# Two transposes inside one pair of products per up stage, and residual additions block by block, in a two-layer encoder

## The chip, the cores and the metric

The kernel runs on one core of one Trainium2 chip. The metric is device time in microseconds, the median of the runs of one kernel. Engines are named as in the profile: PE (TensorE matmul) with PEld (its weight loads), DVE (VectorE), ACT (ScalarE), POOL (GpSimd) and SP (SyncE, which here only issues DMAs).

## The reference, cut to what matters

The program is an encoder trunk of two layers over 256 tokens of width 2048. Each layer is a token mixer and a gated MLP, both added to the residual. The change lies in the MLP alone.

```python
def conv_glu(hn, w_up, conv_w, conv_b, w_down):
    u = hn @ w_up                              # 2048 -> 2 * 5504
    a, v = jnp.split(u, 2, axis=-1)
    ...                                        # width-3 convolution of a along the tokens: c
    return (jax.nn.gelu(c, approximate=False) * v) @ w_down

for layer in range(DEPTH):
    hn = rmsnorm(h, norm_mix_g[layer])
    ...                                        # layer 0: mLSTM mixer, layer 1: HGRN2 mixer
    h = h + mix
    h = h + conv_glu(rmsnorm(h, norm_ffn_g[layer]), ffn_w_up[layer], ffn_conv_w[layer],
                     ffn_conv_b[layer], ffn_w_down[layer])
```

## The kernel before

**Precision.** Every float32 operand is split into a high and a low part (`halves`: L170 on ACT casts the high part `wh`, L171 on DVE subtracts to get the low part `wl`), and a product is a sum of products of parts.

**The MLP in stages.** The 43 blocks of 128 hidden columns are worked in three parts of 16, 16 and 11 blocks (`PARTS`). Part 0, 1 and 2 of a layer each have an *up stage* and then a *down stage*.

**Up stage.** One chunk (kind `fm`) per hidden block, over 16 steps k of the contraction. A step has two blocks of weights, f = 0 (the gate branch) and f = 1 (the value branch), and for each a **pair of products** into one PSUM bank: L441, high weights with 512 moving columns (high and low part of the activations side by side), and L444, low weights with 256 moving columns. A chunk is thus 32 pairs, and an up stage of 16 chunks 512 pairs. PE has nothing else to do in it.

**The `turn` transposes.** At places given by the table `RESETS`, the kernel issues a PE transpose of the identity matrix into a spare bank (`turn`, L428). Nothing reads its result. The table names a chunk of the stage and a step k: chunk 2 and chunk 9 of part 0, chunks 0 and 6 of parts 1 and 2, one transpose each, ahead of a pair.

**Down stage.** Two `Pair` objects, one for each half of the 2048 output columns. A `Pair` multiplies 2x2 blocks by a scheme with seven instead of eight block products (`stream_pair`, products recorded at L309). Its plan is a string such as `PSNSPSNN`: P and S are groups by the scheme, N and H plain products; for S the sums of weights are made on DVE (`T`, L234 to L236), for P they come precomputed from DRAM (`pr`). The products accumulate in two PSUM tiles of two banks, `d0` (its halves are `c12` and `c11`) and `d1` (`c22` and `c21`), and in three banks `m1`, `m6`, `m7`. PSUM holds two such `d` tiles, so the second `Pair` of a stage gets the same two tiles and its first product in `c12` waits until they are read.

**Back into the residual.** After the last scheme group `middle` copies `m1` and `c22` out on ACT (into `s1` and `v5`), forms the remaining sums in a tile `at` on DVE (L1156 to L1158) and adds them to the residual `hx` (L1182, two additions of 1024 columns). `at` is one of the three buffers of the tag `raw`, the same through which the weights arrive from DRAM. At the end of the `Pair`, `done` adds the two `d` tiles to the residual (L1187, two additions of 1024 columns). The last half of the last part uses plain chunks instead of a `Pair`, so there are 11 `Pair`s in all, and the second follows directly on the first in five stages (parts 0, 1, 2 of layer 0; parts 0, 1 of layer 1).

**What sets the order.** The program is built by a tile framework that schedules the instructions of every engine by a simulated timeline and puts in the semaphores. So the order in the source is not the order on an engine, and a change in one place can move instructions in another. Each engine executes its own list in order. SP issues the weight DMAs in order, each when its `raw` buffer is free.

Of the kernel before, what the change touches and what calls it, by code (L numbers as in the profile page):

```python
# [8 lines left out]
F32 = mybir.dt.float32  # L9
# [3 lines left out]
ALU = mybir.AluOpType  # L13
PSUM = bass.MemoryType.PSUM

P = 128
# [2 lines left out]
KT = D // P  # L19
FT = 5504 // P  # L20
PARTS = ((0, 16), (16, 16), (32, 11))
RESETS = (((2, 1), (9, 1)), ((0, 3), (6, 1)), ((0, 3), (6, 1)))
A = "PSNSPSNN"
A2 = "PSNSPSNN"
B = "PSNNNH"
# [24 lines left out]
RAW = 3  # L50
# [15 lines left out]
def trunk_kernel(ctx, tc, xT, x_d, fg_d, pp_d, cst_d, sel_d, w_gate, w_first, w_aq, w_ak, w_av, w_ao, w_aout,  # L66
                 w_bq, w_bv, w_bg, w_bout, w_up, w_down, w_last, out, mscr, sums):
    nc = tc.nc
    act, dve, pool, pe = nc.scalar, nc.vector, nc.gpsimd, nc.tensor

    keep = ctx.enter_context(tc.tile_pool(name="keep", bufs=1))
    wpool = ctx.enter_context(tc.tile_pool(name="wpool", bufs=1))
# [12 lines left out]
    ident = cst[:, C_ID:C_ID + P]  # L85
# [5 lines left out]
    def aux(name):  # L91
        return psa.tile([P, 512], F32, tag="aux", name=name)
# [279 lines left out]
    def stream(chunks):  # L372
        pieces = split_weights(chunks[1:])
        ready = []

        def fetch():
            p = next(pieces, None)
            if p is not None:
                ready.append(p)

        chunks[0].before()
        first_chunk(chunks[0], n0, fetch)
        for ch in chunks[1:]:
            if ch.before:
                ch.before()
            if ch.kind == "pair":
                def take():
                    fetch()
                    return ready.pop(0)
                stream_pair(ch, take)  # L390
                continue
            if ch.apart:
                ps = [aux("mm") for _ in range(2)]
            else:
                d = double("mm")
                ps = [d[:, 0:512], d[:, 512:1024]]
            k = 0
            while k < ch.nk:
                fetch()
                wh, wl, n = ready.pop(0)  # L400
                if ch.last and k + sum(p[2] for p in ready) + n == ch.nk:
                    pieces_, k0 = [(wh, wl, n)] + ready, k
                    for t in range(2):
                        k = k0
                        for wh, wl, n in pieces_:
                            for kk in range(n):
                                x, c = ch.x(k), slice(kk * 512, (kk + 1) * 512)
                                xh, xl = x[:, t * P:(t + 1) * P], x[:, T + t * P:T + (t + 1) * P]
                                pe.matmul(ps[t], xh, wh[:, c], start=False, stop=False)
                                pe.matmul(ps[t], xh, wl[:, c], start=False, stop=False)  # L410
                                pe.matmul(ps[t], xl, wh[:, c], start=False, stop=k == ch.nk - 1)
                                k += 1
                        ch.half(ps[t], t)
                    return
                for kk in range(n):
                    x = ch.x(k)
                    st, sp = k == 0, k == ch.nk - 1
                    if ch.kind != "fm":
                        c = slice(kk * 512, (kk + 1) * 512)
                        for t in range(2):  # L420
                            xh, xl = x[:, t * P:(t + 1) * P], x[:, T + t * P:T + (t + 1) * P]
                            pe.matmul(ps[t], xh, wh[:, c], start=st, stop=False)  # L422
                            pe.matmul(ps[t], xh, wl[:, c], start=False, stop=False)  # L423
                            pe.matmul(ps[t], xl, wh[:, c], start=False, stop=sp)  # L424
                        side.tick(1.3)
                    else:
                        if k == ch.reset:
                            pe.transpose(aux("turn")[:, 0:P], ident, ident)  # L428
                        if k == 1 and ch.turns or side.turned:
                            side.turned = False  # L430
                            cs = [slice(kk * ch.width + f * P, kk * ch.width + (f + 1) * P) for f in range(2)]
                            for f in range(2):
                                pe.matmul(ps[f], wh[:, cs[f]], x, start=st, stop=False)  # L433
                            for f in range(2):
                                pe.matmul(ps[f][:, 0:T], wl[:, cs[f]], x[:, 0:T], start=False, stop=sp)  # L435
                            side.tick(0.65)
                            k += 1
                            continue
                        for f in range(len(ps)):
                            c = kk * ch.width + f * P  # L440
                            pe.matmul(ps[f], wh[:, c:c + P], x, start=st, stop=False)  # L441
                            if f:
                                side.tick(0.325 * len(ps))
                            pe.matmul(ps[f][:, 0:T], wl[:, c:c + P], x[:, 0:T], start=False, stop=sp)  # L444
                    k += 1
            ch.done(ps)
# [643 lines left out]
    def ffn(layer, norm, nxt):  # L1090
# [56 lines left out]
            def form(self, c, kind):  # L1147
                return self.forms[c, kind]

        def combine(acc, at, w):  # L1150
            v5 = ev.tile([P, 512], F32, tag="jk", bufs=1, name="v5")[:, 0:w]
            flat = at.rearrange("p t c -> p (t c)")
            s1, u2, u3 = (flat[:, 512 * i:512 * i + w] for i in range(3))
            act.copy(s1, acc["m1"][:, 0:w])
            act.copy(v5, acc["c22"][:, 0:w])
            dve.tensor_tensor(u2, s1, acc["m6"][:, 0:w], ALU.add)  # L1156
            dve.tensor_tensor(u3, u2, acc["m7"][:, 0:w], ALU.add)
            dve.tensor_tensor(at[:, :, 512:512 + w], flat[:, 512:1536].rearrange("p (a c) -> p a c", a=2)[:, :, 0:w],  # L1158
                              v5.unsqueeze(1).broadcast_to([P, 2, w]), ALU.add)

        for part, (f0, nf) in enumerate(PARTS):
            GT = Gated(nf)
            final = last and part == len(PARTS) - 1
            made = [{} for _ in range(2)]
            ahead = []
            for c in range(1 if final else 2):
                for i, kind in enumerate((DOWN_PLAN, DOWN_PLAN2)[c][nf]):
                    if kind == "P":
                        made[c][i] = numbers.pop()
                        ahead.append((made[c][i], w_down[layer, c][:, (f0 + 2 * i) * 1024:(f0 + 2 * i + 2) * 1024]))  # L1170

            for i in range(nf):
                chunks.append(Chunk("fm", w_up[layer, f0 + i], KT, norm.x, done_up(f0 + i, i, GT, ahead)))
                chunks[-1].reset = dict(RESETS[part]).get(i)
                chunks[-1].apart = bool(part) and i == 0
            for c in (0, 2):
                def middle(acc, c=c):
                    at = wpool.tile([P, 2048], F32, tag="raw", bufs=RAW, name="at").rearrange("p (t c) -> p t c", t=2)
                    combine(acc, at, 512)
                    for t in range(2):  # L1180
                        h = hm[:, t, 512 * c:512 * c + 1024]
                        dve.tensor_tensor(h, h, at[:, t], ALU.add)  # L1182

                def done(acc, c=c, part=part):
                    for t in range(2):
                        h = hm[:, t, 512 * c:512 * c + 1024]
                        dve.tensor_tensor(h, h, acc["rows"][t], ALU.add)  # L1187
                    if part == len(PARTS) - 1:
                        if last or c:
                            end()  # L1190
                        nxt.add(c)
                        nxt.add(c + 1)
                if final and c == 2:
                    continue
                ch = Pair(w_down[layer, c // 2][:, f0 * 1024:(f0 + nf) * 1024], (DOWN_PLAN if c == 0 else DOWN_PLAN2)[nf], GT.get, GT.form, done, middle)
                ch.made, ch.box = made[c // 2], box
                chunks.append(ch)
            if final:
                def done(ps):
                    for t in range(2):  # L1200
                        h = hm[:, t, 1024:1536]
                        dve.tensor_tensor(h, h, ps[t], ALU.add)
                    nxt.add(2)
                for c in (2, 3):
                    chunks.append(Chunk("tm", w_last[c - 2], nf, GT.get, done))
                chunks[-1].last, chunks[-1].half = True, nxt.half
                chunks[-1].apart = chunks[-2].apart = True
# [135 lines left out]
```

## Time and profile before

| | |
|---|---|
| median of 3 runs | 2399.92 us |
| the three runs | 2402.45, 2399.92, 2399.79 us |
| the profiled execution | 2402.44 us, with a span of 2400.4 us from first to last instruction |
| PE busy | 2383.1 us, 99% of the span |
| DVE busy | 1940.4 us, 81% |
| ACT busy | 1338.3 us, 56% |
| mean DMA rate | 226 GB/s over the span |

In the profile a row of the timeline reads: start in us, duration in us, engine, source line, operation, tile written <- tiles read, shape, count; in square brackets the idle time of the engine before it and what ended it. Matmuls are pipelined, so the duration of one is longer than the distance to the next; where rates are meant, the distances between starts are used. A row of the windows view reads: stretch, its length, then per engine the busy time and in brackets the number of instructions, and at the end the granted PE clock, the DMA share and the rate.

### The profile page before, as it was taken

Reading aid. Unit: us, or ns where it says so; the run is one execution under the profiler, and the core shown is the slowest. Engines: PE = TensorE matmul, PEld = TensorE weight load, DVE = VectorE, ACT = ScalarE, POOL = GpSimd, SP = SyncE. Lnnn points to the kernel's source line nnn. Section 1 sums busy time; section 2 is a strip of 40 time slices with the busy share of each in tenths; the row PEclk is TensorE's granted clock in tenths of the full one; section 3 lists DMA queues with packets and bytes.
Section 4 is the critical chain, followed back from the end, with each engine's and each line's share of the span. In section 5 each row is a group of like instructions: output and inputs, shape, how many; then the busy total and the mean of one; then the engine's idle time right before and its main releaser. Section 6 shows DMA issues by size and latency. Waiting matters only on the chain.

```text
span 2400.4 us, 37326 instructions
## 1 busy us (share of the span) xinstructions
PE 2383.1 (99%) x14212; PEld 2037.1 (85%) x14212; DVE 1940.4 (81%) x3197; ACT 1338.3 (56%) x2057; POOL 306.0 (13%) x451
## 2 busy tenths in 40 slices
PE   9999999999999999999999999999999999999998
PEld 7888888888888888888888888888888888887887
DVE  7766655888988888888888888885788888888876
ACT  6655455655556645655555555555565556654554
POOL 0100000111011110101222222220011101110100
PEclk9999999999999999999999999999999999999999
DMA  7655555888778887855455555445698768987854
GB/s 295 203 174 171 191 174 186 272 275 281 268 251 277 287 286 238 292 196 204 172 176 167 168 176 173 165 174 181 223 296 282 262 239 276 293 284 243 260 190 175
DMA packets 106019, 545.84 MB, mean 227 GB/s; under 512 B 10720, under 2 KB 11360, under 8 KB 55280
## 3 DMA queue, kind: packets, MB, share of 16 engines
q1 hardware_dynamic: 66656, 437.34, 53.2%
q0 software_dynamic: 38320, 104.94, 14.5%
q8 instruction: 111, 1.82, 0.3%
q10 hardware_dynamic: 864, 1.19, 0.1%
q14 instruction: 68, 0.56, 0.1%
HBM read 501.41 MB, written 42.01 MB: 226 GB/s over the span
## 4 chain that ended last, share of the span: by engine, by line
PE 96%; DVE 2%; DMA 2%; issue 0%; ACT 0%; SPq 0%; POOLq 0%; POOL 0%; ACTq 0%; DVEq 0%
PE mm L441 36%; PE mm L444 18%; PE c L309 11%; PE mm L422 7%; PE mm L423 7%; PE mm L424 7%; PE m L309 3%; DMA raw<-in_w_down 1%; DVE wl L171 1%; PE mm L433 1%; PE pn L790 1%; PE pd L973 1%; PE py L1022 1%; PE pz L536 0%; PE mm L435 0%
## 5 line engine op out<-in xcount | busy, mean ns | idle before, releaser
L441 PE MATMUL mm<-xt,wh 128*128 128x512 f32 x3690 | 1289.0, 395 | 0.0
L170 ACT CAST wh<-raw 128x1024 fp32r<-128x1024 f32 (+1 forms) x829 | 844.2, 1026 | 794.9 <-PE mm L441 471.7
L171 DVE TENSOR_TENSOR wl<-raw,wh 128x1024 fp32r<-128x1024 f32 (+1 forms) x829 | 989.8, 1199 | 357.8 <-ACT wh L170 351.0
L444 PE MATMUL mm<-xt,wl 128*128 128x256 f32 x3690 | 1027.1, 279 | 0.0
L441 PEld LDWEIGHTS mm<-xt,wh 128*128 128x128 f32 x3690 | 691.8, 188 | 158.4
L444 PEld LDWEIGHTS mm<-xt,wl 128*128 128x128 f32 x3690 | 693.7, 188 | 1.4
L309 PE MATMUL c<-wh,g 128*128 128x512 f32 x666 | 217.5, 390 | 0.0
L422 PE MATMUL mm<-wh,xt 128*128 128x512 f32 x480 | 188.2, 392 | 0.0
L423 PE MATMUL mm<-wl,xt 128*128 128x512 f32 x480 | 187.7, 391 | 0.0
L424 PE MATMUL mm<-wh,xt 128*128 128x512 f32 x480 | 187.3, 390 | 0.0
L309 PEld LDWEIGHTS c<-wh,g 128*128 128x128 f32 x666 | 125.2, 188 | 26.1
L309 PE MATMUL c<-wl,g 128*128 128x512 f32 x333 | 129.9, 390 | 0.0
L424 PEld LDWEIGHTS mm<-wh,xt 128*128 128x128 f32 x480 | 90.2, 188 | 18.5
L422 PEld LDWEIGHTS mm<-wh,xt 128*128 128x128 f32 x480 | 90.1, 188 | 18.5
L423 PEld LDWEIGHTS mm<-wl,xt 128*128 128x128 f32 x480 | 90.2, 188 | 17.4
L476 ACT COPY b<-mm 128x256 f32<-128x256 f32 x236 | 86.4, 366 | 20.5 <-DVE z L477 6.7
L170 ACT CAST wh<-T 128x1024 fp32r<-128x1024 f32 x54 | 55.3, 1050 | 69.7 <-PE c L309 43.3
L262 POOL DMA_DIRECT2D sums<-pr x76 | 53.0, 699 | 293.9 <-ACT pr L259 156.2
L282 POOL DMA_DIRECT2D pr<-sums x76 | 41.3, 551 | 359.5 <-PE c L309 244.5
L171 DVE TENSOR_TENSOR wl<-T,wh 128x1024 fp32r<-128x1024 f32 x54 | 64.8, 1223 | 26.0 <-ACT wh L170 25.7
L249 POOL COPY pr<-a 128x1 f32<-128x1 f32 x38 | 31.1, 819 | 424.2 <-DVE a L482 246.6
L309 PE MATMUL c<-wh,F 128*128 128x512 f32 x178 | 70.2, 394 | 3.8 <-DVE hx L1187 3.8
(274 smaller groups left out, 3022.7 us busy)
## 6 DMA issues: line engine op xcount, KB each, us to landing
raw<-in_w_up SPq DMA_DIRECT2D x172, 1024.0 KB, 5.6
raw<-in_w_down SPq DMA_DIRECT2D x60, 1024.0 KB, 6.1
raw<-in_w_bq SPq DMA_DIRECT2D x48, 1024.0 KB, 4.9
sums<-pr POOLq DMA_DIRECT2D x76, 512.0 KB, 8.1
pr<-sums POOLq DMA_DIRECT2D x76, 512.0 KB, 7.5
pr<-in_w_down POOLq DMA_DIRECT2D x38, 512.0 KB, 6.7
raw<-in_w_ao SPq DMA_DIRECT2D x16, 1024.0 KB, 4.9
raw<-in_w_aout SPq DMA_DIRECT2D x16, 1024.0 KB, 4.8
```

The lines of the kernel that those rows point to most:

```text
L170: act.copy(h, r)
L171: dve.tensor_tensor(l, r, h.bitcast(F32), ALU.subtract)
L249: pool.tensor_copy(b[:, 0, 0:1], after)
L262: pool.dma_start(sums[n, j].rearrange("p (i o b) -> p i o b", i=2, o=2)[:, :, o], v.rearrange("p (i b) -> p i b", i=2))
L282: pool.dma_start(z[j], sums[n, j][:, 1024 * i:1024 * i + 1024])
L309: pe.matmul(o, a, b, start=name not in begun, stop=sp and i == 2)
L422: pe.matmul(ps[t], xh, wh[:, c], start=st, stop=False)
L423: pe.matmul(ps[t], xh, wl[:, c], start=False, stop=False)
L424: pe.matmul(ps[t], xl, wh[:, c], start=False, stop=sp)
L441: pe.matmul(ps[f], wh[:, c:c + P], x, start=st, stop=False)
L444: pe.matmul(ps[f][:, 0:T], wl[:, c:c + P], x[:, 0:T], start=False, stop=sp)
L476: act.copy(b, ps[:, T:2 * T])
```

## The change

In the up stage the table `RESETS` now names one place per part: chunk 2, step 1 in part 0 (as the first entry before), and chunk 0, step 0 in parts 1 and 2. There, two transposes are issued instead of one, after the high product of f = 0 and ahead of its low product, both into one `turn` tile. Two transposes stood in each up stage before (at two places), and two stand there now.

In the down stage, `middle` does without `combine`: the sums are formed and added to the residual in blocks of 512 columns, eight additions of 512 in place of two of 512, one of 2x512 and two of 1024. In `done`, the two halves of `d0` are added each by itself, `c12` first, then `c11`; `d1` is added as a whole as before.

```diff
-RESETS = (((2, 1), (9, 1)), ((0, 3), (6, 1)), ((0, 3), (6, 1)))
+RESETS = ((2, 1), (0, 0), (0, 0))
...
-                        if k == ch.reset:
-                            pe.transpose(aux("turn")[:, 0:P], ident, ident)
...
                             pe.matmul(ps[f], wh[:, c:c + P], x, start=st, stop=False)
                             if f:
                                 side.tick(0.325 * len(ps))
+                            if not f and k == ch.reset:
+                                turn = aux("turn")
+                                for o in (0, P):
+                                    pe.transpose(turn[:, o:o + P], ident, ident)
                             pe.matmul(ps[f][:, 0:T], wl[:, c:c + P], x[:, 0:T], start=False, stop=sp)
...
-        def combine(acc, at, w):
-            v5 = ev.tile([P, 512], F32, tag="jk", bufs=1, name="v5")[:, 0:w]
-            flat = at.rearrange("p t c -> p (t c)")
-            s1, u2, u3 = (flat[:, 512 * i:512 * i + w] for i in range(3))
-            act.copy(s1, acc["m1"][:, 0:w])
-            act.copy(v5, acc["c22"][:, 0:w])
-            dve.tensor_tensor(u2, s1, acc["m6"][:, 0:w], ALU.add)
-            dve.tensor_tensor(u3, u2, acc["m7"][:, 0:w], ALU.add)
-            dve.tensor_tensor(at[:, :, 512:512 + w], flat[:, 512:1536].rearrange("p (a c) -> p a c", a=2)[:, :, 0:w],
-                              v5.unsqueeze(1).broadcast_to([P, 2, w]), ALU.add)
...
                 def middle(acc, c=c):
-                    at = wpool.tile([P, 2048], F32, tag="raw", bufs=RAW, name="at").rearrange("p (t c) -> p t c", t=2)
-                    combine(acc, at, 512)
-                    for t in range(2):
-                        h = hm[:, t, 512 * c:512 * c + 1024]
-                        dve.tensor_tensor(h, h, at[:, t], ALU.add)
+                    at = wpool.tile([P, 2048], F32, tag="raw", bufs=RAW, name="at")
+                    s1, u2, u3 = (at[:, 512 * i:512 * i + 512] for i in range(3))
+                    v5 = ev.tile([P, 512], F32, tag="jk", bufs=1, name="v5")
+                    h11, h12, h21, h22 = (hm[:, t, o:o + 512] for t in range(2) for o in (512 * c, 512 * c + 512))
+                    add = lambda o, a, b: dve.tensor_tensor(o, a, b, ALU.add)
+                    act.copy(s1, acc["m1"])
+                    act.copy(v5, acc["c22"])
+                    add(u2, s1, acc["m6"])
+                    add(h11, h11, s1)
+                    add(u3, u2, acc["m7"])
+                    add(u2, u2, v5)
+                    add(h21, h21, u3)
+                    add(u3, u3, v5)
+                    add(h12, h12, u2)
+                    add(h22, h22, u3)
 
                 def done(acc, c=c, part=part):
-                    for t in range(2):
-                        h = hm[:, t, 512 * c:512 * c + 1024]
-                        dve.tensor_tensor(h, h, acc["rows"][t], ALU.add)
+                    for name, t, o, n in (("c12", 0, 512, 512), ("c11", 0, 0, 512), ("rows", 1, 0, 1024)):
+                        h = hm[:, t, 512 * c + o:512 * c + o + n]
+                        dve.tensor_tensor(h, h, acc["rows"][1] if n == 1024 else acc[name], ALU.add)
```

What the scheduler made of it is seen at three places. The first is PE in part 0 of layer 0, at the end of step 0 and the start of step 1 of chunk 2; `xt_3112` and `xt_3115` are the activations of steps 0 and 1. Before:

```order
L441 MATMUL mm<-xt_3112,wh 128x512
L444 MATMUL mm<-xt_3112,wl 128x256
L428 MATMUL turn<-cst 128x128
L441 MATMUL mm<-xt_3115,wh 128x512
L444 MATMUL mm<-xt_3115,wl 128x256
L441 MATMUL mm<-xt_3115,wh 128x512
```

With the change (L439 and L446 are the two products, L445 the transposes):

```order
L439 MATMUL mm<-xt_3112,wh 128x512
L446 MATMUL mm<-xt_3112,wl 128x256
L439 MATMUL mm<-xt_3115,wh 128x512
L445 MATMUL turn<-cst 128x128 x2
L446 MATMUL mm<-xt_3115,wl 128x256
L439 MATMUL mm<-xt_3115,wh 128x512
```

The transposes moved from between two pairs into a pair, and there are two. The second single transpose of this stage, at chunk 9, is gone. It is the same in layer 1.

The second place is PE at the start of the up stage of part 1 in layer 0, where the last products of the down stage of part 0 (L309) end. Before, the scheduler had drawn both transposes of the stage together and put them behind two high products:

```order
L309 MATMUL c_5788<-wh,g_5459 128x512
L441 MATMUL mm<-xt_3112,wh 128x512 x2
L428 MATMUL turn<-cst 128x128 x2
L444 MATMUL mm<-xt_3112,wl 128x256 x2
L441 MATMUL mm<-xt_3115,wh 128x512
L444 MATMUL mm<-xt_3115,wl 128x256
```

With the change:

```order
L309 MATMUL c_5791<-wh,g_5458 128x512
L439 MATMUL mm<-xt_3112,wh 128x512
L445 MATMUL turn<-cst 128x128 x2
L439 MATMUL mm<-xt_3112,wh 128x512
L446 MATMUL mm<-xt_3112,wl 128x256 x2
L439 MATMUL mm<-xt_3115,wh 128x512
L446 MATMUL mm<-xt_3115,wl 128x256
```

The two transposes now stand one high product earlier, so two low products follow each other without them. Part 2 and layer 1 read the same.

The third place is DVE around the change from the first `Pair` to the second in part 0 of layer 0. `m_...` and `c_...` are the PSUM tiles of the first `Pair`; `wl<-raw` are low parts of weights of both, `T` the sums for the second. Before:

```order
L1158 TENSOR_TENSOR at<-at,v_5711 128x2x512
L171 TENSOR_TENSOR wl<-raw,wh 128x1024
L1182 TENSOR_TENSOR hx<-hx,at 128x1024 x2
L171 TENSOR_TENSOR wl<-raw,wh 128x512
L234 TENSOR_TENSOR T_5801<-raw 128x1024
L1187 TENSOR_TENSOR hx<-hx,c_5462 128x1024
L1187 TENSOR_TENSOR hx<-hx,c_5463 128x1024
L235 TENSOR_TENSOR T_5801<-raw,T_5801 128x512
```

With the change (L1173 are the additions of `middle`, L1188 those of `done`):

```order
L1173 TENSOR_TENSOR hx<-hx,at 128x512 x2
L171 TENSOR_TENSOR wl<-raw,wh 128x1024
L1173 TENSOR_TENSOR at<-at,v_5710 128x512
L171 TENSOR_TENSOR wl<-raw,wh 128x512
L234 TENSOR_TENSOR T_5804<-raw 128x1024
L1173 TENSOR_TENSOR hx<-hx,at 128x512
L1188 TENSOR_TENSOR hx<-hx,c_5461 128x512 x2
L235 TENSOR_TENSOR T_5804<-raw,T_5804 128x512
L1188 TENSOR_TENSOR hx<-hx,c_5462 128x1024
```

Most additions of `middle` moved ahead of the weights that arrive at the change of `Pair`s; one of them stands behind the sum `T`; and the addition of the second `d` tile moved behind the second step of `T`.

More of the change, by code (lines that the diff above doesn't have):

```diff
@@ L1173, in ffn @@
                 chunks.append(Chunk("fm", w_up[layer, f0 + i], KT, norm.x, done_up(f0 + i, i, GT, ahead)))
[L1174 removed]
+                chunks[-1].reset = RESETS[part][1] if i == RESETS[part][0] else None
                 chunks[-1].apart = bool(part) and i == 0
```

## The prediction

> **What bounds the kernel now.** I read first the page, for the busiest engine and for the chain that ended last.
>
> ```profile
> span 2400.4 us, 37326 instructions
> PE 2383.1 (99%) x14212; PEld 2037.1 (85%) x14212; DVE 1940.4 (81%) x3197; ACT 1338.3 (56%) x2057; POOL 306.0 (13%) x451
> PE 96%; DVE 2%; DMA 2%; issue 0%; ACT 0%; SPq 0%; POOLq 0%; POOL 0%; ACTq 0%; DVEq 0%
> ```
>
> PE is busy for 99% of the span. A change that issues the same products can win only by making their distance in time smaller, or by ending one of PE's few waits. So the next view is the windows of the up stages with the high products (L441) alone. One such product starts each pair, so the length of a window over its count is the time of a pair.
>
> ```profile
> 418.20:495.60 77.40, 77.40 (x224) 41.81 (x223) 1.00 0.86 272
> 495.90:574.10 78.20, 78.20 (x222) 41.53 (x221) 1.00 0.87 283
> 656.90:833.60 176.70, 176.62 (x510) 95.44 (x510) 1.00 0.85 275
> 916.40:1037.70 121.30, 121.15 (x350) 65.51 (x350) 1.00 0.80 265
> 1710.80:1788.15 77.35, 77.35 (x224) 41.79 (x223) 1.00 0.86 270
> 1788.50:1866.70 78.20, 78.20 (x222) 41.53 (x221) 1.00 0.86 284
> ```
>
> A row reads: window; its length; PE busy with the count; PEld with the count; granted clock; DMA share; GB/s. The first and the second window are one stage, part 0 of layer 0, with the same work in all pairs. The first has 345.5 ns a pair, the second 352.3 (one pair of each count is cut by the window's start). Parts 1 and 2 (third and fourth row) are at 346.5 and 346.6. Layer 1 repeats it. The clock is 1.00 in all. So PE has two paces for the same pair, and only the second stretch of part 0 is slow. The timeline shows what stands at the border:
>
> ```profile
> 417.87 0.27 PE L428 MATMUL turn<-cst 128*128 128x128 f32 x1
> ...
> 495.28 0.40 PE L441 MATMUL mm<-xt,wh 128*128 128x512 f32 x1
> 495.51 0.28 PE L444 MATMUL mm<-xt,wl 128*128 128x256 f32 x1
> 495.63 0.27 PE L428 MATMUL turn<-cst 128*128 128x128 f32 x1
> 495.66 0.48 PE L441 MATMUL mm<-xt,wh 128*128 128x512 f32 x1
> ...
> 496.10 0.40 PE L441 MATMUL mm<-xt,wh 128*128 128x512 f32 x1
> ...
> 573.83 0.40 PE L441 MATMUL mm<-xt,wh 128*128 128x512 f32 x1
> ```
>
> From 496.10 to 573.83, the last pair of the stage, lie 220 pairs: 77.73 / 220 = 353.3 ns, or 6.7 more than 346.6. The single transpose at 417.87 left the pace fast; the second, at 495.63, is followed by the slow pace until the stage ends. The same transpose thus can leave either pace, and what decides is finer than the source. That is the main uncertainty here.
>
> The other idle time is at the change from one `Pair` to the next:
>
> ```profile
> PE c L309 <- DVE hx L1187: 3.8, 4, 1.1
> ```
>
> Four waits of 3.8 us in all for the addition of `done` that frees the banks of `c11` and `c12`.
>
> **The change, part by part. First the transposes.** Twelve stood in the program and twelve stand there now, so their own time (at most 0.12 us each, the distance from one product to the next) cancels. What counts is the pace they leave.
>
> Part 0: the transpose at chunk 9 goes, so the stage keeps the pace that chunk 2 leaves. If that is fast, 222 pairs gain 6.7 ns in each layer: 222 x 6.7 = 1.49 us, 3.0 us for both. If chunk 2 now leaves the slow pace, the first 224 pairs lose as much and the last stay slow: +1.5 a layer, +3.0 in all.
>
> Parts 1 and 2: before, the two transposes stood together behind two high products, and left the fast pace in all four stages. Now they stand one product earlier. Fast again costs 0; slow costs (510 + 350) x 6.7 = 5.76 us a layer, 11.5 us in both.
>
> No transposes stand inside a pair in this trace. The nearest rows are the mixer's eight products of `py`, also issued between a high and a low product:
>
> ```profile
> 1163.76 0.39 PE L441 MATMUL mm<-xt,wh 128*128 128x512 f32 x1
> 1163.99 1.05 PE L1022 MATMUL py<-V,AT 128*128 128x128 f32 x8
> ...
> 1165.35 0.40 PE L441 MATMUL mm<-xt,wh 128*128 128x512 f32 x1
> ...
> 1167.78 0.40 PE L441 MATMUL mm<-xt,wh 128*128 128x512 f32 x1
> ```
>
> ```profile
> 1300.91 0.40 PE L441 MATMUL mm<-xt,wh 128*128 128x512 f32 x1
> 1301.15 1.05 PE L1022 MATMUL py<-V,AT 128*128 128x128 f32 x8
> ...
> 1302.85 0.40 PE L441 MATMUL mm<-xt,wh 128*128 128x512 f32 x1
> ...
> 1304.97 0.40 PE L441 MATMUL mm<-xt,wh 128*128 128x512 f32 x1
> ```
>
> After the first, 7 pairs take 2.43 us, 347 ns each: fast. After the second, 6 take 2.12 us, 353 ns: slow. The second was entered with 0.24 us from the high product to `py`, the first with 0.23. So an interruption inside a pair can leave either pace too. I take fast for both places as the likeliest: all four stages with two transposes side by side are fast now. The slow prices stay as rivals. Term: -3.0 us, between -3.0 and +14.5.
>
> **Then the additions.** Prices on DVE come from the second change of `Pair`s:
>
> ```profile
> 870.90 1.23 DVE L171 TENSOR_TENSOR wl<-raw,wh 128x1024 fp32r<-128x1024 f32 x1 [2.71 <-ACT wh L170]
> ...
> 874.32 0.68 DVE L171 TENSOR_TENSOR wl<-raw,wh 128x512 fp32r<-128x512 f32 x1
> 874.92 1.22 DVE L234 TENSOR_TENSOR T<-raw 128x1024 f32<-128x1024 f32 x1
> 876.05 2.34 DVE L1187 TENSOR_TENSOR hx<-hx,c 128x1024 f32<-128x1024 f32 x2
> ```
>
> ```profile
> 873.36 1.57 ACT L170 CAST wh<-raw 128x1024 fp32r<-128x1024 f32 x2 [1.97 <-PE c L309]
> ```
>
> ```profile
> 877.32 0.50 PE L309 MATMUL c<-wh,F 128*128 128x512 f32 x1 [1.05 <-DVE hx L1187]
> ```
>
> From start to start, 512 columns take 0.60 us and 1024 take 1.13: two halves cost 0.07 more than a whole. The Trainium skill ("VectorE: DVE Perf Modes", "The TRN2 errata — SBUF-src ops pay a fixed extra latency per instruction") says that every small VectorE instruction repeats a fixed latency, and advises long ones, so it speaks against splitting. The trace agrees, at 0.07 us a cut; 44 more instructions would be 3 us of DVE, little of it in front of PE.
>
> What stands in front of PE's product? Before: L234, one whole L1187, then 0.14 us to PE: 1.13 + 1.13 + 0.14 = 2.40 = 877.32 - 874.92. After: L234, one L1173 of 512, and both halves of `d0`, since `c11` and `c12` are one tile and PE's product waits for both: 1.13 + 3 x 0.60 + 0.14 = 3.07, or 0.67 more. Against that, L234 starts earlier: three of the four additions to `hx` moved ahead of the weights, into the 2.71 us that DVE idles before 870.90. There remain one L171, one L1173 of 512 and one L171 of 512: 870.90 + 1.13 + 0.60 + 0.60 = 873.23. The weights for `T` are there by 873.36, when their cast starts. PE then starts at 873.36 + 3.07 = 876.43: a gain of 0.89.
>
> The other three changes, with the landing as the gate:
>
> ```profile
> 614.64 1.57 ACT L170 CAST wh<-raw 128x1024 fp32r<-128x1024 f32 x2 [2.85 <-DMA raw<-in_w_down]
> 1907.08 1.57 ACT L170 CAST wh<-raw 128x1024 fp32r<-128x1024 f32 x2 [2.62 <-PE c L309]
> ```
>
> ```profile
> 617.72 0.50 PE L309 MATMUL c<-wh,F 128*128 128x512 f32 x1 [0.97 <-DVE hx L1187]
> 1910.40 0.50 PE L309 MATMUL c<-wh,F 128*128 128x512 f32 x1 [1.08 <-DVE hx L1187]
> 2167.19 1.52 PE L309 MATMUL m<-pr,F 128*128 128x512 f32 x6
> 2171.12 0.50 PE L309 MATMUL c<-wh,F 128*128 128x512 f32 x1 [0.74 <-DVE hx L1187]
> ```
>
> ```profile
> 2168.71 1.23 DVE L234 TENSOR_TENSOR T<-raw 128x1024 f32<-128x1024 f32 x1 [1.07 <-DMA raw<-in_w_down]
> ```
>
> 614.64 + 3.07 = 617.71: gain 0. 1907.08 + 3.07 = 1910.15: gain 0.25. At 2168 the weights came late and L234 already waited for them: 0.67 worse in this execution; landing as at 1900, it gains 0.25. The last step is `c2`: its bank is freed behind L235 and a whole addition, 0.60 + 1.13 = 1.73 us after `d0`, while the seven products ahead of it take 7 x 0.226 = 1.58 ((1.52 - 0.39) / 5 is the pitch): 0.15 a time, 0.6 in all. Also `at`, a weight buffer, is released later, behind L234. SP's queue has two weight loads there: the first waited for `at` (to 874.32 in the second change), the second for the L171 behind it (to 874.92). Now the first waits for that L171 (873.23), the second for `at` (873.36 + 1.13 + 0.60 = 875.09): one starts 1.1 us earlier, one 0.2 later, and since both go over the same queues I cost that at nothing; if each counts by itself, the later one's 0.2 a time. Sum with a landing in time: -0.89 - 0.25 - 0.25 + 0.6 = -0.8, rounded to **-1.0**, as the split groups also free ACT's sources sooner. Bounds: -3.8 (all four waits gone), and 4 x (0.67 + 0.15) = +3.3.
>
> **A stretch that is not the change's.** The profiled execution has 2402.44 us, the other two runs about 2399.85. The difference is found at the fourth change:
>
> ```profile
> 2168.50:2171.92 3.42, 1.51 (x5) 0.86 (x5) 3.21 (x3) 1.57 (x2) 0.00 (x0) 1.00 0.94 369
> 2171.92:2175.34 3.42, 3.42 (x10) 2.67 (x9) 3.42 (x6) 1.14 (x2) 0.36 (x1) 0.50 0.49 206
> ```
>
> PE was busy for 1.51 of 3.42 us, then had half the clock for 3.42 us: 1.7 lost there, and 0.9 of idle time above the other changes' 1.0: 2.6 us. The Trainium skill ("TensorE: Matmul & The Clock Gate", "What's actually happening") has a free-running window of 3413 ns and the half clock after an idle one. The trace agrees on the length; but here the window was not idle, so a long wait was enough.
>
> Sum: 2402.44 - 2.6 (not to recur) - 3.0 - 1.0 = 2395.8, **2396 us**.
>
> **The rivals.**
> - *Part 0 falls slow at chunk 2.* For it: one of the two quoted interruptions inside a pair does that. Against it: the transpose at the same step left it fast. 2396 + 6.0 = 2402.
> - *Parts 1 and 2 fall slow, in both layers.* This is the slower side. Place: the first pair of each of these stages; price 11.5 us; it decides once about 1300 of the 1720 pairs are slow. For it: the new order is untried. Against it: two transposes two products later left the fast pace four times. 2396 + 11.5 = 2407.5; with part 0 too, 2413.5.
> - *The additions do not free the banks sooner, as the change says*, because PE waits for both halves: +3.3 instead of -1.0, and two waits long enough for half clock, 2 x 1.7: 2396 + 4.3 + 3.4 = 2403.7.
>
> **How the numbers follow.** A difference of 0.2% (4.8 us; 2395.1 and 2404.7 are the bounds) is about what can be told from no change here. Chances: the forecast 0.50 (its own range 2393.5 to 2398.5: with -3.5 in place of -1.0, or with the half clock again), of which I put 0.24 below 2395.1; part 0 slow 0.24, of which 0.02 beyond 2404.7; parts 1 and 2 slow 0.10; both 0.11; the additions 0.05. So faster 0.24; same 0.26 + 0.22 + 0.05 = 0.53; slower 0.02 + 0.10 + 0.11 = 0.23. The range is 2393.5 to 2408.5: it leaves out the last rival but one and little at the lower end.
>
> **What would show it.** Right: windows of 346.6 ns a pair from the transposes to the end of every up stage; PE's waits for `hx` at the four changes down from 3.8 us to about 2.5. Wrong: any up stage at 353 ns; a wait of 1.7 us there, or a new one on L235's follower; PEclk 0.50 after one of them. If parts 1 and 2 read 353, the forecast is wrong by 11 us and nothing else can make it good.

## The result, and the profile after

The changed kernel takes 2414.11 us (median of 6 runs, 2412.15 to 2415.58) where the kernel before takes 2400.80 (6 runs, the three from before the change among them): a ratio of 1.0054, with a 95% interval of 1.0041 to 1.0067. It is slower, by about 13 us. The profiled execution has a span of 2413.8 us. The page, with the rows that answer to those shown of before:

```profile
span 2413.8 us, 37368 instructions
PE 2397.8 (99%) x14212; PEld 2043.7 (85%) x14212; DVE 1944.0 (81%) x3241; ACT 1337.6 (55%) x2057; POOL 301.1 (12%) x451
PE 96%; DMA 2%; DVE 1%; issue 0%; ACT 0%; SPq 0%; POOLq 0%; POOL 0%; ACTq 0%; DVEq 0%
```

PE has the same 14212 instructions and is busy 14.7 us longer. The windows of the high product (now L439) show where. The columns are as before: window; length; PE busy with the count; PEld with the count; clock; DMA share; GB/s.

```profile
420.60:577.10 156.50, 156.50 (x444) 83.24 (x443) 1.00 0.85 274
659.70:664.10 4.40, 4.38 (x13) 2.34 (x13) 1.00 1.04 389
665.10:839.30 174.20, 174.13 (x494) 92.64 (x493) 1.00 0.83 271
927.40:1046.40 119.00, 118.93 (x338) 63.20 (x338) 1.00 0.80 260
1720.80:1877.90 157.10, 156.92 (x445) 83.44 (x444) 1.00 0.85 275
1964.80:2140.20 175.40, 175.33 (x497) 93.14 (x498) 1.00 0.83 270
2227.00:2345.90 118.90, 118.83 (x338) 63.10 (x337) 1.00 0.71 234
```

Length over count is about 352 to 353 ns everywhere but in the second row (ends of windows cut a pair; inside, the distance is 353.3 ns). All six up stages are slow, at full clock. But parts 1 and 2 do not start slow. The second row is the start of part 1: 12 pairs there have a mean of 347.2 ns. The slow pace begins later, here:

```profile
664.23 0.39 PE L439 MATMUL mm<-xt,wh 128*128 128x512 f32 x1
664.46 0.27 PE L446 MATMUL mm<-xt,wl 128*128 128x256 f32 x1
664.58 0.63 PE L439 MATMUL mm<-xt,wh 128*128 128x512 f32 x2
665.04 0.40 PE L446 MATMUL mm<-xt,wl 128*128 128x256 f32 x2
```

Two high products and then two low ones: the scheduler has swapped two neighbours. The same swap stands at the same place in the kernel before, where the pace stayed fast through it:

```profile
661.41 0.39 PE L441 MATMUL mm<-xt,wh 128*128 128x512 f32 x1
661.64 0.28 PE L444 MATMUL mm<-xt,wl 128*128 128x256 f32 x1
661.76 0.63 PE L441 MATMUL mm<-xt,wh 128*128 128x512 f32 x2
662.22 0.40 PE L444 MATMUL mm<-xt,wl 128*128 128x256 f32 x2
```

The rows round to 0.01 us. In nanoseconds, the trace has the distances from start to start below (B a high product, S a low one, T a transpose; the number is the distance from the one ahead). Part 1 of layer 0, the swapped products with what surrounds them:

```
before  S+230 B+117 S+230 B+116 S+230 B+117 | B+230 S+233 S+125 | B+117 S+233 B+117 S+231 B+112 S+233 B+117 S+231 B+113
after   S+231 B+112 S+233 B+117 S+231 B+112 | B+233 S+231 S+113 | B+119 S+234 B+117 S+241 B+120 S+236 B+113 S+233 B+117
```

There are thus three patterns. **Fast 1**: low to high in 117, 117, 116 ns (the trace has whole nanoseconds, so this may be one value), high to low in 230; 346.6 ns a pair. **Fast 2**: low to high alternates between 112 or 113 and 117 or 118; also 346.6. **Slow**: 113, 117, 120, and high to low up to 241; 353.3. In the kernel before, the stage was in fast 1 ahead of the swap and in fast 2 behind it. In the changed kernel it was in fast 2 ahead, and slow behind.

Counted by these prices, part 0 lost 224 pairs x 6.7 = 1.5 us, part 1 495 x 6.7 = 3.3 and part 2 335 x 6.7 = 2.2 in each layer: 14.0 us. The lengths of the six up stages, from first to last product, say the same: 956.2 us in sum against 942.2. The spans differ by 13.4. The rest is small and of both signs. The additions' wait is a microsecond shorter, and the stretch at half clock behind the fourth change of `Pair`s did not come again. But another stretch at half clock came in this execution, at 15.0 us, long before anything that was changed:

```profile
11.59:15.00 3.41, 1.56 (x6) 0.74 (x6) 1.61 (x4) 2.18 (x5) 0.00 (x0) 1.00 1.04 392
15.00:18.42 3.42, 3.42 (x10) 2.68 (x9) 3.38 (x6) 3.42 (x8) 0.00 (x0) 0.50 1.05 399
```

(Window; length; PE, PEld, DVE, ACT, POOL busy with counts; clock; DMA share; GB/s.) Counted product by product, PE is 0.4 us behind the kernel before at 13.5 us and 1.9 us behind at 18.3. The first up stage begins 1.9 us later.

The four waits at the changes of `Pair`s, and DVE and PE at the first:

```profile
PE c L309 <- DVE hx L1188: 2.8, 4, 1.5
```

```profile
617.45 1.22 DVE L234 TENSOR_TENSOR T<-raw 128x1024 f32<-128x1024 f32 x1
618.59 0.69 DVE L1173 TENSOR_TENSOR hx<-hx,at 128x512 f32<-128x512 f32 x1
619.19 1.28 DVE L1188 TENSOR_TENSOR hx<-hx,c 128x512 f32<-128x512 f32 x2
```

```profile
620.61 0.47 PE L309 MATMUL c<-wh,F 128*128 128x512 f32 x1 [0.41 <-DVE hx L1188]
```

From L234's start to PE's product it is 3.16 us (3.07 were worked out), and the wait is 0.41 instead of about 1.0. The four waits are 0.41, 1.48, 0.49 and 0.46 us, where they were 0.97, 1.05, 1.08 and 0.74.

### The profile page after: what moved, and what is told of

Its sections match the earlier page's. It is cut to its first block, busy times and chain, and to the rows that moved or that the text cites. A ratio compares the mean times of both kernels' runs of the same rounds, so it can differ in the third digit from the quotient of the medians.

```text
span 2413.8 us, 37368 instructions
## 1 busy us (share of the span) xinstructions
PE 2397.8 (99%) x14212; PEld 2043.7 (85%) x14212; DVE 1944.0 (81%) x3241; ACT 1337.6 (55%) x2057; POOL 301.1 (12%) x451
## 4 chain that ended last, share of the span: by engine, by line
PE 96%; DMA 2%; DVE 1%; issue 0%; ACT 0%; SPq 0%; POOLq 0%; POOL 0%; ACTq 0%; DVEq 0%
PE mm L439 36%; PE mm L446 18%; PE c L309 11%; PE mm L422 7%; PE mm L423 7%; PE mm L424 7%; PE m L309 3%; DMA raw<-in_w_down 1%; PE mm L431 1%; PE pn L792 1%; DVE wl L171 1%; PE pd L975 1%; PE py L1024 1%; PE pz L538 0%; PE mm L433 0%
## 5 line engine op out<-in xcount | busy, mean ns | idle before, releaser
L439 PE MATMUL mm<-xt,wh 128*128 128x512 f32 x3690 | 1303.9, 398 | 0.4 <-issue 0.4
L446 PE MATMUL mm<-xt,wl 128*128 128x256 f32 x3690 | 1035.1, 281 | 0.0
L439 PEld LDWEIGHTS mm<-xt,wh 128*128 128x128 f32 x3690 | 692.7, 188 | 166.4 <-issue 0.7
L446 PEld LDWEIGHTS mm<-xt,wl 128*128 128x128 f32 x3690 | 696.4, 189 | 1.6
L309 PE MATMUL c<-wh,g 128*128 128x512 f32 x666 | 217.6, 390 | 0.0
L309 PEld LDWEIGHTS c<-wh,g 128*128 128x128 f32 x666 | 125.0, 188 | 25.9
L309 PE MATMUL c<-wl,g 128*128 128x512 f32 x333 | 129.6, 389 | 0.0
L422 PEld LDWEIGHTS mm<-wh,xt 128*128 128x128 f32 x480 | 90.1, 188 | 18.3
L309 PEld LDWEIGHTS c<-wl,g 128*128 128x128 f32 x333 | 62.5, 188 | 13.3
```

The lines of the kernel that those rows point to most:

```text
L309: pe.matmul(o, a, b, start=name not in begun, stop=sp and i == 2)
```

## The experiments

Theory A at the start: the loss is the pace of the pairs alone, set by where an interruption falls in the pattern. Rivals: the additions did it (Q), or an interruption inside a pair leaves the slow pace as such (R).

**Each half of the change alone.** The first kernel has `combine`, `middle` and `done` of before with the transposes of the change; the second the reverse.

```diff
-                    add(u2, s1, acc["m6"])
-                    add(h11, h11, s1)
-...
+                    combine(acc, at, 512)
+                    for t in range(2):
+                        h = hm[:, t, 512 * c:512 * c + 1024]
+                        dve.tensor_tensor(h, h, at[:, t], ALU.add)
```

> The transposes as in the change, the additions as before. Theory A (the pace of the pairs): all of the loss is in the up stages, so all six read about 353 ns a pair from the 17th pair of parts 1 and 2 and from chunk 2 of part 0 on, and the waits for hx stay at 3.8 us in sum: 2400.8 + 14.5 = 2415.3 us. Rival Q (the additions move the scheduler's order and with it the pace): parts 1 and 2 stay at 346.6 ns and the time is 2398 to 2401 us.

Measured: 2414.75 us, ratio 1.0054 (1.0041 to 1.0068). All six stages slow from the same places on.

> The additions as in the change, the transposes as before. Theory A: paces as before (only the second half of part 0 slow, parts 1 and 2 at 346.6 ns), the waits for hx down from 3.8 to about 2.8 us: about 2399.8 us, no difference that can be told. Rival Q: 2412 to 2415 us.

Measured: 2398.66 us, ratio 0.9992 (0.9983 to 1.0001). The up stages read as before; part 1 of layer 0:

```profile
656.50:832.60 176.10, 176.02 (x509) 95.17 (x508) 1.00 0.86 278
```

So the whole loss belongs to the transposes; Q falls. By medians the additions gain 2.2 us, and the interval just reaches 1: at most what a measurement here can just tell.

**One pair later.** The same two transposes, in the second pair of the step.

```diff
-                            if not f and k == ch.reset:
+                            if f and k == ch.reset:
```

> The change with one thing different: the two transposes stand in the second pair of the step (f = 1) instead of the first (f = 0). On PE, parts 1 and 2 then begin with two high products, two transposes, two low products, as before the change; in part 0 the transposes come one pair later. Theory A (the place within the alternating pattern of distances decides): parts 1 and 2 stay at 346.6 ns; in part 0 the transposes are entered after a high product that follows its forerunner by 0.11 us instead of 0.12, and leave the fast pace to the stage's end: 2400.8 - 3.0 - 1.0 = 2396.8 us. Rival R (two transposes between a high and a low product leave the slow pace wherever they stand): part 0 slow from chunk 2 on, 2400.8 + 3.0 - 1.0 = 2402.8 us.

Measured: 2396.87 us, ratio 0.9981 (0.9973 to 0.9990), faster than both kernels. Its windows from behind the transposes to the end of each stage:

```profile
419.00:572.00 153.00, 153.00 (x442) 82.47 (x441) 1.00 0.86 279
654.70:831.00 176.30, 176.22 (x509) 95.20 (x509) 1.00 0.85 278
913.70:1034.50 120.80, 120.72 (x349) 65.22 (x349) 1.00 0.81 270
1708.70:1861.90 153.20, 153.20 (x443) 82.66 (x442) 1.00 0.86 279
1946.00:2122.20 176.20, 176.12 (x509) 95.17 (x508) 1.00 0.84 278
2204.80:2325.60 120.80, 120.72 (x349) 65.23 (x349) 1.00 0.74 243
```

All six stages fast, 346 ns. Only the place of the transposes differs, by one pair, and in part 0 they still stand between a high and a low product. R falls. Part 0, in nanoseconds:

```
change   B+112 S+233 B+117 S+231 B+112 S+233 B+117 | T+238 T+108 | S+29 B+204 S+230 B+117 S+234 B+117 S+241 B+120   slow
one on   B+117 S+231 B+113 S+232 B+118 S+231 B+112 | T+234 T+110 | S+29 B+200 S+234 B+116 S+235 B+117 S+230 B+117   fast 1
```

**A second interruption in each stage.** The table gives each stage of each layer its own places (chunk, step, f, number of transposes, input); the added transposes read a weight tile so that the scheduler can't draw them ahead. Nothing reads their results.

```diff
-RESETS = ((2, 1), (0, 0), (0, 0))
+RESETS = ((((2, 1, 0, 2, 0), (5, 1, 1, 2, 1)), ((0, 0, 0, 2, 0), (3, 1, 0, 2, 1)), ((0, 0, 0, 2, 0), (3, 1, 1, 2, 1))),
+          (((2, 1, 1, 1, 0), (5, 1, 0, 2, 1)), ((0, 0, 0, 2, 0), (3, 2, 0, 2, 1)), ((0, 0, 0, 2, 0), (3, 1, 1, 1, 1))))
...
-                                    pe.transpose(turn[:, o:o + P], ident, ident)
+                                    pe.transpose(turn[:, o * P:o * P + P], wh[:, c:c + P].bitcast(F32) if pin else ident, ident)
```

> The change with a second interruption in each up stage, at another place in each, held there by taking a weight tile as the transposes' input: layer 0 part 0 after 96 further pairs, two transposes in a pair of f = 1; layer 0 part 1 after 80 pairs, two in f = 0; layer 0 part 2 after 81 pairs, two in f = 1; layer 1 part 0 one transpose in f = 1 first (one pair later than the change), then after 94 pairs two in f = 0; layer 1 part 1 after 82 pairs, two in f = 0; layer 1 part 2 after 81 pairs, one in f = 1. Theory A (a state that an interruption moves on, by the place where it falls): some of these return a slow stage to 346.6 ns, and places one pair apart differ; each stage that returns saves 1.7 to 2.8 us, and layer 1 part 0 is fast between its two interruptions. Rival R (an interruption inside a pair leaves the slow pace): all stay at 353 ns and the time is that of the change, 2414 us.

Measured: 2407.71 us in one run. Before and behind the second place in parts 0 and 1 of layer 0, then behind it in part 1 of layer 1:

```profile
419.00:451.50 32.50, 32.50 (x93) 17.29 (x92) 1.00 0.72 235
453.50:573.50 120.00, 120.00 (x347) 64.70 (x346) 1.00 0.89 288
662.00:690.50 28.50, 28.43 (x82) 15.10 (x81) 1.00 0.66 218
692.50:834.30 141.80, 141.80 (x410) 76.48 (x409) 1.00 0.89 285
...
1987.00:2131.00 144.00, 144.00 (x409) 76.61 (x408) 1.00 0.86 280
```

Two slow stages came back to the fast pace (353.3 ns, then 346.7, by the distances inside the windows): once with f = 1, once with f = 0. Three stayed slow. Layer 0 part 1 and layer 1 part 1 differ, beside the layer, only in that the second interruption falls two pairs later, and one is fast, the other slow. Part 0 of layer 1, one transpose in f = 1, was fast, and still fast behind its second place. So neither f nor the number alone decides. That the place in the pattern does is what is left; this run does not show it.

**Without transposes.**

```diff
-                chunks[-1].reset = RESETS[part][1] if i == RESETS[part][0] else None
+                chunks[-1].reset = None
```

> The change without any transposes in the up stages. Theory A: part 0 comes in fast from its first chunks and has nothing that moves it on: 346.6 ns to its end. Parts 1 and 2 begin in an order of their own on PE (a product swapped with its neighbour at three places within the first 17 pairs) and so may settle in either pace: 2396.9 us if fast, 2396.9 + 11.5 = 2408.4 us if slow. Rival T (it is the transposes that bring the fast pace): part 0 slow too, 2414.4 us.

Measured: 2404.49 us, ratio 1.0014 (1.0005 to 1.0023). Parts 0, 1 and 2 of layer 0:

```profile
399.60:571.90 172.30, 171.82 (x497) 92.91 (x496) 1.00 0.83 271
658.40:833.70 175.30, 175.23 (x497) 93.12 (x496) 1.00 0.83 271
920.60:1039.40 118.80, 118.73 (x337) 63.06 (x336) 1.00 0.79 260
```

Part 0 is fast to its end with no transposes; the second transpose of the kernel before was what slowed it. Parts 1 and 2 are slow from their last swapped products on. Rival T falls for part 0, while parts 1 and 2, in an order with three swaps each, are slow without transposes. By the ratios, the kernel with no transposes is (1.0054 - 1.0014) x 2400 = 9.6 us faster than the change. In the profiles, 7.2 us of this lie in the up stages (949.0 us against 956.2): 6.0 are the 445 pairs of part 0 at 6.7 ns in two layers, and about 1.2 are the twelve transposes themselves, 0.2 for each two. The rest lies outside the up stages and is not explained.

**The additions again, beside the better transposes.** The kernel with f = 1 with the additions of before, and once more as it was.

> The transposes in the second pair of the step (f = 1), two of them, with the additions as before the change. Theory A: all six up stages at 346.6 ns, since the additions do not touch the pace; beside the kernel with the same transposes and the split additions only the waits for hx differ. If the split additions are worth what the runs with the old transposes showed (about 2 us), this is about 2398.9 us; if they are worth nothing, 2396.9 us.

> The transposes in the second pair of the step and the split additions, once more, beside the same with the old additions on one chip: about 2396.9 us, all six up stages at 346.6 ns.

Measured on one chip: 2397.96 us with the old additions (ratio 0.9989, 0.9980 to 0.9998) and 2397.22 with the split ones (0.9983, 0.9974 to 0.9991). All stages fast in both. 0.7 us is not told from nothing. The profiles agree in sign: PE waited for `hx`

```profile
PE c L309 <- DVE hx L1189: 3.7, 4, 1.2
```

with the old additions, and

```profile
PE c L309 <- DVE hx L1188: 2.6, 3, 1.5
```

with the split ones. But the sum moves by more than that from execution to execution: with the old additions the other profiles have 3.8 and 5.4 us, with the split ones 1.6 to 4.2.

**The rule by distances, tested.** The refined theory named an outcome for each of six other places (an input of 2 takes the low part of the weight tile).

```diff
-RESETS = ((2, 1), (0, 0), (0, 0))
+RESETS = ((((2, 2, 0, 2, 0),), ((0, 0, 0, 2, 0), (0, 4, 1, 1, 2)), ((0, 0, 0, 2, 0), (0, 4, 0, 1, 2))),
+          (((2, 1, 0, 1, 0),), ((0, 0, 1, 1, 0),), ((0, 0, 1, 2, 0), (2, 1, 0, 2, 1))))
```

> Other places and numbers of transposes in the split-addition kernel, one per up stage. Theory A, refined: in the fast pattern whose low-to-high distances alternate between 0.117 and 0.112 us, an interruption behind a high product that came 0.117 us after its forerunner turns the pace slow, one behind 0.112 keeps it fast, whether one transpose or two, f = 0 or f = 1. Layer 0 part 0 (two, one step later than the change, 0.117): slow. Layer 1 part 0 (one only, at the change's place, 0.117): slow. Layer 0 part 2 (the change's two at the start, and one more behind the 7th following pair's high product, 0.112): fast to the end, as the swapped products at the 17th pair then only move one fast pattern to the other. Layer 0 part 1 (the same, but one pair later, 0.117): slow up to the swapped products, open after them. Layer 1 part 1 (one transpose at the start, in f = 1): fast. Layer 1 part 2 (two in f = 1 at the start, and two more 48 pairs after the swapped products, in f = 0, 0.112): fast to the end. Time 2396.9 + 3.0 + 3.0 = 2402.9 us, and 3.3 more if layer 0 part 1 stays slow. Rival R (two transposes in f = 0 leave slow, one or f = 1 fast): layer 1 part 0 fast, layer 1 part 2 slow from its second place on.

Measured: 2408.12 us in one run. Behind the last place of each stage (for the last stage, ahead of its second place too):

```profile
419.50:575.30 155.80, 155.80 (x442) 82.86 (x441) 1.00 0.85 274
661.50:834.30 172.80, 172.72 (x499) 93.33 (x499) 1.00 0.85 275
919.80:1038.00 118.20, 118.12 (x342) 63.87 (x341) 1.00 0.81 266
1712.60:1869.00 156.40, 156.40 (x444) 83.19 (x443) 1.00 0.85 274
1957.20:2132.50 175.30, 175.23 (x497) 93.12 (x496) 1.00 0.83 270
2215.20:2237.00 21.80, 21.73 (x63) 11.54 (x62) 1.00 0.78 275
2239.00:2338.40 99.40, 99.40 (x282) 52.82 (x282) 1.00 0.71 232
```

Right were both stages of part 0 (slow, one transpose or two) and layer 0 part 2 (fast), though this last one came there by another way: it was slow from its start, and the added transpose brought it back. Three of six were wrong. Layer 0 part 1 should have been slow up to the swapped products and is fast: its added transpose followed a high product at 118 ns and still left fast 1. Layer 1 part 1, with one transpose at the start, began in fast 2 and turned slow at the swapped products. And layer 1 part 2 was slow from its first pairs, with the same instructions in the same order as in the kernel with f = 1. Its row, and that of f = 1:

```profile
2214.62 0.38 PE L446 MATMUL turn<-cst 128*128 128x128 f32 x2
2214.76 0.48 PE L447 MATMUL mm<-xt,wl 128*128 128x256 f32 x2
```

```profile
2204.33 0.38 PE L445 MATMUL turn<-cst 128*128 128x128 f32 x2
2204.46 0.48 PE L446 MATMUL mm<-xt,wl 128*128 128x256 f32 x2
```

In nanoseconds, the first transpose came 237 after the high product in the mixture, and 230 in the other. Layer 0 part 2 is a second such case: it has the start of the change, which led to fast 2 there, entered at 233 in place of 230, and was slow. So the refined rule (117 slow, 112 fast) holds for transposes of the identity in part 0 and not beyond. The places that broke it inside a stage also had another input, a weight tile, and the two are not told apart here.

**Is it the execution or the program?** Both mixtures once more, unchanged.

> The third mixture once more, unchanged. Theory A (the order of the instructions settles the pace): the same stages fast and slow as in its first run, layer 1 part 2 slow from its start included, 2408 us. Rival E (an execution can fall either way at the same instructions): layer 1 part 2, whose start is word for word that of the kernel with the transposes in f = 1, starts fast this time, which saves 2.4 us or, if it turns slow at its second place, 0.3.

> The second mixture once more, unchanged. Theory A: the same stages fast and slow as in its first run, 2407.7 us. Rival E: at least one stage differs, by 1.7 to 3 us.

Measured, on another chip than at first: 2407.20 and 2403.68 us (the kernel before takes 2399.95 there, in one run). In each of the twelve stages the pace is what it was in the first run, and changes at the same place. For the odd stage of the third mixture, again slow from its start:

```profile
2214.30:2236.10 21.80, 21.73 (x63) 11.56 (x62) 1.00 0.78 273
2238.10:2337.50 99.40, 99.40 (x282) 52.81 (x282) 1.00 0.71 233
```

Rival E falls: in these two programs the pace comes with the program, not with the execution. The second mixture's two times differ by 4 us with the same paces in all stages; 2.6 of it are waits for `hx` (4.2 and 1.6 us), which depend on when weights land.

**What held in every profile.** Swapped products stand in steady pairs at 52 places of the twelve profiles. (Three kernels are among these profiles twice.) From fast 1 they led to fast 2 in 24 of 24, from fast 2 to slow in 22 of 22, from slow to fast 2 in 4 and to slow in 2. That is why the change lost parts 1 and 2. Its two transposes stand one product earlier, so the stage begins in fast 2 instead of fast 1, and the swap 17 pairs on, which was there before and did no harm, takes it to slow.

The third mixture also shows this by an intervention. Its part 1 of layer 0 begins as in the change, in fast 2. One more transpose, ahead of the swap, brings it to fast 1, and the same swap then leaves it fast, in both executions:

```
S+231 B+113 S+232 B+118 | T+233 | S+27 B+200 S+235 B+116 S+230 B+117 ... S+230 B+117 | B+230 S+233 S+124 | B+118 S+232 B+118 S+231 B+112
```

What the transposes themselves leave goes with the distance at which they were entered. At 80 places of the twelve profiles a transpose follows a high product. All 40 that came 230 or 231 ns after it left a fast pace, all 14 that came 237 ns or more after it left the slow one, and of the 26 between 18 left a fast pace and 8 the slow one. This distance is itself measured only with the transpose in place, so it is a sign of the state and not shown to be its cause.

## Why the prediction was wrong

- **Forecast 2396, range to 2408.5, measured 2414.1.** The case that came, both places slow, was among the rivals with 2413.5 us and a chance of 0.11, and beyond the range's end.
- **The step that failed** is "I take fast for both places as the likeliest: all four stages with two transposes side by side are fast now". In place of its -3.0 us, the up stages cost +14.0: part 0 was slow from the transposes on (3.0), parts 1 and 2 from the swapped products on (11.0). Fast 1 and fast 2 have the same time per pair, and the prediction's windows cannot tell them apart. In parts 1 and 2, the state that the transposes left mattered not for the pairs at once behind them, but for what the swapped products made of it.
- **The rival's place was wrong, its price nearly right.** It put the loss in "the first pair of each of these stages". It began at the 17th pair. The term was 11.5 us for parts 1 and 2, and 11.0 were found (3.3 + 2.2 a layer); for part 0 it was 3.0, and 3.0 were found. That swap is in the order of both kernels; the prediction spoke of it nowhere.
- **Part 0.** "The second was entered with 0.24 us from the high product" was the right thing to look at: the change's transposes were entered at 238 ns and slowed the pace, those one pair on at 234 and did not. The row was quoted and then not followed to the pattern ahead of the transposes, which could have been read at 417.87 in the trace of before. In nanoseconds, the two interruptions that the prediction quotes differ as these two places do: the one that stayed fast was entered at 231, behind a high product that followed its forerunner by 113, and the one that turned slow at 235, behind 117. The change's place in part 0 is behind 117.
- **"If that is fast, 222 pairs gain 6.7 ns in each layer":** the mechanism was right. With f = 1, and with no transposes, part 0 is fast to its end. With f = 1 the up stages take 939.2 us against 942.2 before, the 3.0 us of the term, and the kernel takes 2396.87 us, within a microsecond of the 2396 that the sum gives where all stages are fast.
- **The additions: -1.0 us.** The three profiles with the old additions have 3.8, 5.4 and 3.7 us of waits for `hx`, the change 2.8 us and the others with the split ones 1.6 to 4.2. The times are 0.7 us (with f = 1) to 2.2 (with the old transposes) apart. The sign is the same in both pairs, and the size can't be told better. The term of 0.6 us for `c2` was not found: behind L234 only one wait stands at each change in the profile of the change. The rival in which the additions cost 3.3 us is refuted by the time of the additions alone: 0.9992 with an upper end of 1.0001, where 3.3 us would be 1.0014. That they free the banks sooner at every change is not shown, as one of the four waits grew.
- **The half clock, 2.6 us, "not to recur".** The change's profile has none at the changes of `Pair`s, though PE waited up to 1.5 us there; its half clock is the one at 15.0 us, shown above. At the fourth change it came again in one other profile, the second of the kernel with f = 1, behind the same late landing:

```profile
2163.80:2167.20 3.40, 1.87 (x7) 1.05 (x6) 3.40 (x6) 0.88 (x2) 0.00 (x0) 1.00 0.97 347
2167.30:2170.70 3.40, 3.40 (x10) 2.69 (x9) 3.40 (x5) 1.42 (x2) 1.06 (x2) 0.52 0.46 193
```

  So it belongs to the execution, and counting it out of the likeliest time was right, calling it done with was not. PE was busy for 1.87 of 3.40 us ahead of it. The Trainium skill ("TensorE: Matmul & The Clock Gate", "What's actually happening") asks for an idle window ahead of half clock. Three profiles here show half clock behind a window in which PE was busy for 1.51 to 1.87 of about 3.4 us, and the measurement decides. But the busy time alone does not settle it. In the kernel with the transposes alone, on the grid of 3.41 us that its own two clock changes give, a window with 1.61 us, ahead of which and in which PE waited for 2.2 us at a stretch, was followed by full clock, and what makes the difference stays open:

```profile
1918.33:1921.74 3.41, 1.61 (x7) 1.35 (x8) 3.41 (x5) 0.57 (x1) 0.00 (x0) 1.00 0.87 336
1921.74:1925.15 3.41, 3.41 (x17) 2.70 (x15) 3.41 (x5) 1.37 (x2) 2.12 (x4) 1.00 0.92 332
```

## What to carry to other kernels

Two stretches with the same time per product need not be in the same state, and an interruption that is harmless in one can cost 2% of a stage's time in the other. So before instructions are put into a steady stream of matmuls, read the distances from start to start in nanoseconds over one period ahead of the place, list every later irregularity in the stream, and try the neighbouring place too: one pair on, the same two transposes with the same additions made -4 us of +13. The reading alone does not replace the run: of six outcomes that were named from the distances, three were wrong.

## What was not expected of the hardware

- The same two products, at the same granted clock of 1.00, have three steady patterns of distances (346.6, 346.6 and 353.3 ns a pair) that last for hundreds of pairs, until something interrupts them.
- The outcome of an interruption repeats from execution to execution to the place (twelve of twelve stages, on two chips each), though each execution has its own waits ahead of it.
- It does not follow from the order of PE's instructions alone: the same start of a stage was entered at 230 ns in one program and at 237 in another, and ended fast in the one and slow in the other; a second start, entered at 230 and at 233, did the same. What in the program makes these few ns was not found and stays open.
- The same program differs by up to 6 us between runs (2394.35 to 2400.28 with f = 1, whose two profiles have all stages fast). The profiles place part of it at the changes of `Pair`s: 2.6 us of waits in one pair of runs, and a stretch at half clock in one profile of f = 1 that the other has not.
